# Self-attention over ragged batches on one core: V projected by key blocks, second halves that project one class lower, one class more, and a table for the SP queue

## The chip, the cores and the metric

The kernel runs on one core of a Trainium2 chip. The time is the device time of one launch in microseconds, the median of the runs shown. Before the change it is 361.95 us, the median of three runs from 361.56 to 365.25 us. Engines are called as the profile calls them: PE is TensorE's matmul, PEld its weight load, DVE VectorE, ACT ScalarE, POOL GpSimd, SP SyncE, which here only issues DMAs.

## The reference

Thirty-two batches of up to 512 rows with 512 features have a length each, drawn between 64 and 511. Rows past the length come out as zero. Eight heads of 64 features attend within a batch.

```python
for b in range(batch):                       # 32
    seq_len = lengths[b]
    x_b = x[b, :seq_len]
    q, k, v = np.split(x_b @ w_qkv, 3, axis=-1)          # w_qkv: 512 x 1536
    # heads of 64: (8, seq_len, 64) each
    scores = scale * q @ k.transpose(0, 2, 1)
    attn = exp(scores - max); attn = attn / (attn.sum(-1) + 1e-08)
    output[b, :seq_len] = (attn @ v).transpose(1, 0, 2).reshape(seq_len, 512)
```

## The kernel before, in words

The lengths are in device memory, so the program is compiled for any of them. At its start it sorts the batches by length, longest first, and takes them in sixteen pairs. Each pair gets a class, which is the smallest multiple of 32 from 64 to 512 that holds its longer batch. For every class N there is one compiled body for a whole pair (`make_body`), written out instruction by instruction for PE, ACT and DVE, and `loops` lays the bodies one behind the other: each engine compares the class of the next pair with k, and runs body k as often as the class repeats, or jumps past it. T is the number of 128-row tiles, the ceiling of N / 128.

With the lengths of this case (502, 447, 446, 436, 363, ... 75) the pairs of before have the classes 512, 448, 384, 352, 352, 352, 320, 288, 256, 224, 224, 192, 160, 160, 128 and 96. So there are four batches of four tiles, twelve of three, twelve of two and four of one.

A body has two halves, h = 0 and 1, one for each batch of the pair. In half h the kernel attends in batch h and at the same time projects the next batch, which has the buffers g = 1 - h (`half`). The order of work in a half is a string of tokens in `ORDER`, or `DENSE` for a three-tile class with 3N up to 1024. Each token issues one group of matmuls on PE and the instruction that empties their PSUM bank:

- S: scores of one head pair, `scores` (D: all three key tiles at once, `scores_dense`). Two heads of a pair have 64 rows of the array each. ACT takes the exponential into `ep`. Head pairs 1, 2 and 3 of batch h come first, and pair 0 of the next batch last, so the first scores of a half have been made in the half before.
- Q, K, B: projection of q, k or both for one head pair of the next batch (`qk`): four matmuls of N columns for each. A capital lets DVE copy the result into `qkT`, a small letter lets ACT do so.
- V: projection of v (`vproj`): for one head pair, for all T tiles, four matmuls of 128 columns per tile. DVE multiplies by the row mask into `v_aug`.
- A: attention times v, `attnv`, 128 rows of the batch at a time, 65 columns each; DVE follows with the reciprocal and the multiplications into `onat`.
- O, P: ACT stores one half of the output columns. SP stores the other where there is no P.

Projections alternate between two PSUM banks (`pa`, banks a0 and a1), scores between two others (s0 and s1). PE acquires a bank by a semaphore that the emptying instruction raises. The matmuls of a pair are 2 x 256 for four tiles, 2 x 176 for three (184 where dense), 2 x 112 for two and 2 x 52 for one; with 168 in the prologue and 8 in a bridge ahead of the one-tile classes these are all 4896 of the trace, so that every half can be found in it by counting.

The SP queue carries, for each half (`body` under `block.sync`): wait until `xT[h]` is free, T transposes of `x16[h]` into `xT[h]`, wait for the cast, the load of the batch five ranks ahead as T x 128 rows, zero fills of output rows, and for three and four tiles the second output store. The batch number comes from register loads of `idx` (`batch_of`). POOL casts `x_nat` to `x16` and writes the column of ones in `v_aug`.

`fetch_far` gives PE a hint, ahead of time, whether the next class's body will run or be jumped past.

Of the kernel before, what the change touches and what calls it, by code (L numbers as in the profile page):

```python
# [9 lines left out]
I32 = mybir.dt.int32  # L10
AF = mybir.ActivationFunctionType
ALU = mybir.AluOpType
# [7 lines left out]
CLASSES = [32 * k for k in range(16, 1, -1)]  # L20
# [34 lines left out]


class Matmuls:


    def __init__(self, mms, raises):  # L60
        self.todo = [(mm, raises.get(k, [])) for k, mm in enumerate(mms)]

    def __call__(self, e):
        for mm, sems in self.todo:
            ins = mm(e)
            for sem in sems:
                ins.then_inc(sem, 1)

# [39 lines left out]
def kernel(  # L108
# [51 lines left out]
    cls = sb("cls", [1, B // 2 + 1], I32)  # L160
    idx = sb("idx", [1, NR], I32)
    n_s = sb("n_s", [P, NR], FP32)
# [28 lines left out]
    s_cls = sem("s_cls")  # L191
    s_x0 = [sem(f"s_x0{t}") for t in range(NT)]
# [15 lines left out]
    s_xtf = [sem(f"s_xtf{h}") for h in range(2)]  # L208
    s_x16f = [sem(f"s_x16f{h}") for h in range(2)]
# [19 lines left out]
    def close(pr, b, eng, mms):  # L229
# [4 lines left out]
        pr.add("pe", Matmuls(mms, raises))  # L234
# [124 lines left out]
    def vproj(pr, bank, h, i, T):  # L359
        b = f"a{bank}"  # L360
        mms = []
        if T == 1:
# [14 lines left out]
        for t in range(T):  # L377
            for c in range(NC):
# [14 lines left out]
                in1=now[0][:, 0, 0:T].unsqueeze(2).unsqueeze(3).broadcast_to([P, T, 2, HD]),  # L393
                op=ALU.mult,
# [3 lines left out]
    def attnv(pr, h, i, T, late=False):  # L398
# [46 lines left out]
        def recip():  # L445
            pr.take("dve", full[("av", "dve")])
            pr.add("dve", lambda e: e.reciprocal(out=rv, in_=den).then_inc(s_r, 1))  # L447

        def mult():
            for j in (0, 1) if T == 1 else (i // 2,) if T != 4 or i % 2 == 0 else ():  # L450
                pr.take("dve", s_od[h][j], 16)
            pr.take("dve", s_r)

# [35 lines left out]
    def spread_last(pr):  # L489
# [14 lines left out]
    }  # L504
    DENSE = "D Q0 K0 A0 V0 D Q1 A1 k1 V1 D Q2 K2 A2 V2 D Q3 A3 k3 V3 O"

    ahead = {}

    def read_class(pr, h):
        if h == 0:  # L510
            for g in ("pe", "act", "dve"):
                pr.add(g, lambda e: next_class(e))

    def fetch_far(pr, h, N):

        k = CLASSES.index(N)
        if h == 0 and k + 2 < len(CLASSES):

            def hint(e):
                cur, far = regs[e.engine][1], regs["far"]  # L520
                e.reg_alu(far, cur, k + 2, ALU.is_lt)
                ahead[k + 1] = e.mark_branch_hint_location(far)

            pr.add("pe", hint)

    def half(pr, h, T, N, st):

        g = 1 - h
        pr.signals += [s_vf[g]] if T == 1 else [s_xtf[h], s_vf[g]]
# [7 lines left out]
        if T == 1:  # L537
            start_proj()
            qk(pr, st["bank"], g, [(i, 0) for i in range(NPAIR)], N, P)
            qk(pr, st["bank"] ^ 1, g, [(i, 1) for i in range(NPAIR)], N, P, "act")  # L540
            read_class(pr, h)
            pr.take("pe", s_on[h])
            attnv(pr, h, 0, 1)
            vproj(pr, st["bank"], g, 0, 1)
            fetch_far(pr, h, N)
            acquire(pr, f"a{st['bank'] ^ 1}")
            pr.signals.append(s_xtf[g])
            scores(pr, h, g, 0, 0, 1, N)
            act_store(pr, h, 0, T)
# [5 lines left out]
        dense = T == 3 and 3 * N <= 2 * MAXS  # L555
        toks = (DENSE if dense else ORDER[T]).split()
        for tok in toks:
# [3 lines left out]
            if k == "S":  # L561
                i, kt = units.pop(0)
                scores(pr, st["slot"], g if i == 0 else h, i, kt, T, N)
                st["slot"] ^= 1
            elif k == "D":
                i = units[0][0]
                del units[:T]
                scores_dense(pr, g if i == 0 else h, i, N)
# [9 lines left out]
            elif k in "OP":  # L578
                act_store(pr, h, "OP".index(k), T)
            else:  # L580
                start_proj()
                eng = "act" if k.islower() else "dve"
                if k == "V":
                    vproj(pr, st["bank"], g, i, T)
                elif k in "Bb":
                    qk(pr, st["bank"], g, [(i, 0), (i, 1)], N, 256, eng)
# [660 lines left out]
```

## Time and profile before

| | |
|---|---|
| median of the runs | 361.95 us |
| profiled execution, span | 359.8 us, granted clock 0.995 |
| median less span | 2.15 us |
| PE busy | 341.4 us, 4896 matmuls |
| DVE busy | 232.2 us |
| ACT busy | 228.3 us |
| POOL busy | 60.8 us |
| DMA | 76.18 MB, mean 212 GB/s |
| last matmul | starts at 352.70 us, ends at 352.90 us |
| last output store issued | 353.79 us, lands at 357.5 us |

The profiled execution is one run; its span goes from the first to the last instruction, and what is launched around it is the 2.15 us of the third row. A share of busy time is a mean over stages. A line of a group says how long its instructions ran and, behind the bar, how long the engine was idle ahead of them and who ended that. In the table by stretches each engine has its busy time in that stretch, with the count of instructions in brackets.

### The profile page before, as it was taken

The page shows a single profiled execution, that of the slowest core. Times are in us where ns is not written, and L with a number is a line of the kernel's source. Part 1 is how long each engine was busy: PE and PEld are TensorE (multiplying, and loading weights), DVE is VectorE, ACT ScalarE, POOL GpSimd, SP SyncE. Part 2 cuts the span into 40 slices and gives each one's busy share as a digit, 9 for nine tenths or more (in the row PEclk, how much of TensorE's full clock was granted, in tenths as well). Part 3 has the DMA queues.
Part 4 walks back from the last instruction along what each step waited for, and adds up shares of the span by engine and source line. Part 5 has one row for each costly group of instructions (what it writes and reads, how often), then busy time and mean ns, then how long its engine had stood idle before and what let it go on. Part 6 is the DMA issues. An engine that isn't in the chain of part 4 may idle for free. (4 is left out here: it accounts for less than half of the span.)

```text
span 359.8 us, 12852 instructions
## 1 busy us (share of the span) xinstructions
PE 341.4 (95%) x4896; PEld 246.9 (69%) x4897; DVE 232.2 (65%) x534; ACT 228.3 (63%) x299; POOL 60.8 (17%) x90
## 2 busy tenths in 40 slices
PE   6999999899989999999999999999999999999892
PEld 2566556566656667666666677788879898888761
DVE  3666666566657677676676766576756666676562
ACT  4668778677757667666676667666666565555441
POOL 2614010202010111011011011101112112212120
PEclk9999999999999999999999999999999999999997
DMA  6968998769668766989759749878896856887664
GB/s 196 379 175 272 220 298 229 195 203 171 207 166 237 192 221 202 238 254 293 215 156 318 226 120 305 263 163 192 210 237 180 162 181 161 208 164 215 169 167 111
DMA packets 85127, 76.18 MB, mean 212 GB/s; under 512 B 41552, under 2 KB 64080, under 8 KB 85072
## 3 DMA queue, kind: packets, MB, share of 16 engines
q1 hardware_dynamic: 69952, 60.78, 66.0%
q10 hardware_dynamic: 15120, 14.68, 12.6%
q8 instruction: 33, 0.54, 0.6%
q14 instruction: 22, 0.18, 0.2%
HBM read 29.37 MB, written 36.70 MB: 184 GB/s over the span
## 5 line engine op out<-in xcount | busy, mean ns | idle before, releaser
L290 ACT ACTIVATE ep<-psc 128x704 f16<-128x704 f32 (+4 forms) x217 | 173.9, 852 | 73.8 <-PE psc L248 54.7
L248 PE MATMUL pa<-xT,w_r 128*128 128x352 f16 (+11 forms) x1056 | 164.5, 284 | 1.6 <-DVE qkT L709 0.5
L357 DVE CAST qkT<-pa 128x352 f16<-128x352 f32 (+5 forms) x152 | 85.3, 562 | 58.5 <-PE pa L248 56.6
L248 PEld LDWEIGHTS pa<-xT,w_r 128*128 128x128 f16 x1056 | 82.5, 98 | 45.1 <-issue 19.3
L248 PE MATMUL pa<-w_r,xT 128*128 128x128 f16 (+1 forms) x1296 | 94.9, 221 | 2.1 <-DVE v_aug L390 1.7
L248 PEld LDWEIGHTS pa<-w_r,xT 128*128 128x128 f16 x1296 | 77.2, 98 | 18.1 <-issue 6.3
L248 PE MATMUL pav<-v_aug,ep 128*128 128x65 f16 x1792 | 79.8, 194 | 3.5 <-issue 2.9
L248 PEld LDWEIGHTS pav<-v_aug,ep 128*128 128x128 f16 x1792 | 72.1, 98 | 15.9 <-issue 4.5
L390 DVE TENSOR_TENSOR v_aug<-pa,masks 128x384 f16<-128x384 f32 (+2 forms) x116 | 60.8, 524 | 34.1 <-PE pa L248 29.8
L248 PE MATMUL psc<-qkT 64*128 64x352 f16 (+12 forms) x688 | 66.2, 292 | 1.2 <-PEq L48 1.0
L471 DVE SCALAR_TENSOR_TENSOR onat<-pav,masks,rcp 128x256 f32<-128x256 f32 (+2 forms) x128 | 51.8, 444 | 6.0 <-DVEq L48 1.9
L1119 POOL CAST v_aug<-masks 128x24 f16 (+4 forms) x33 | 9.1, 275 | 267.6 <-POOLq L900 267.6
L1114 POOL CAST x<-x_nat 128x1536 f16<-128x1536 f32 (+3 forms) x33 | 42.1, 1274 | 11.1 <-POOLq L900 10.5
L322 ACT ACTIVATE ep<-psc 128x960 f16<-128x960 f32 (+1 forms) x32 | 28.0, 928 | 16.0 <-PE psc L248 13.5
L248 PEld LDWEIGHTS psc<-qkT 64*128 64x128 f16 x688 | 23.0, 94 | 19.0 <-issue 9.4
L355 ACT CAST qkT<-pa 128x320 f16<-128x320 f32 (+4 forms) x36 | 17.4, 482 | 27.4 <-ACTq L48 17.3
L447 DVE RECIPROCAL rcp<-pav 128x8 f32<-128x8 f32 (+1 forms) x68 | 14.5, 214 | 13.5 <-PE pav L248 10.0
L469 DVE TENSOR_TENSOR onat<-pav,rcp 128x512 f32<-128x512 f32 (+2 forms) x32 | 17.8, 558 | 1.1
L658 PE MATMUL psc<-zt 128*128 128x512 f16 x22 | 6.7, 456 | 1.7 <-DVE zt L1179 1.7
L1125 POOL MEMSET ep<- 128x1024 f32 x6 | 5.4, 955 | 7.4 <-DVE x L719 7.4
L728 ACT CAST w_r<-w_f 128x512 f16<-128x512 f32 (+1 forms) x6 | 4.4, 758 | 3.3 <-DMA w_f<-in_w_qkv_dram 3.3
L658 PEld LDWEIGHTS psc<-zt 128*128 128x128 f16 x22 | 2.3, 113 | 4.3 <-issue 1.7
(58 smaller groups left out, 31.7 us busy)
## 6 DMA issues: line engine op xcount, KB each, us to landing
out_dram<-zt SPq DMA_DIRECT2D x16, 768.0 KB, 6.2
x_nat<-in_x_dram SPq DMA_DIRECT2D x12, 768.0 KB, 5.1
x_nat<-in_x_dram SPq DMA_DIRECT2D x7, 1024.0 KB, 6.7
out_dram<-onat ACTq DMA_DIRECT2D x28, 256.0 KB, 3.7
x_nat<-in_x_dram SPq DMA_DIRECT2D x12, 512.0 KB, 4.2
out_dram<-onat ACTq DMA_DIRECT2D x12, 384.0 KB, 3.3
out_dram<-onat SPq DMA_DIRECT2D x12, 384.0 KB, 3.6
x_nat<-in_x_dram SPq DMA_DIRECT2D x12, 256.0 KB, 3.7
```

The lines of the kernel that those rows point to most:

```text
L248: return lambda e: e.matmul(o, lhsT, rhs, start=start, stop=stop)
L290: lambda e: e.activation(out=dst, in_=src, func=AF.Exp, scale=scale),
L322: lambda e, par=par, b=b: e.activation(out=ep[:, i, par, 0:3, 0:N], in_=psc_f[:, par, 0 : 3 * N].rearrange("p (t n) -> p t n", n=N), func= ...
L355: group(pr, b, eng, mms, lambda e: e.copy(out=dst, in_=src))
L357: group(pr, b, eng, mms, lambda e: e.tensor_copy(out=dst, in_=src))
L390: lambda e: e.tensor_tensor(out=v_aug[h][:, 0:T, 2 * i : 2 * i + 2, 0:HD], in0=pa[:, bank, 0 : T * P].rearrange("p (t a d) -> p t a d", a= ...
L447: pr.add("dve", lambda e: e.reciprocal(out=rv, in_=den).then_inc(s_r, 1))
L469: ins = e.tensor_tensor(op=ALU.mult, **ops)
L471: ins = e.scalar_tensor_tensor(scalar=now[0][:, 1, t : t + 1], op0=ALU.mult, op1=ALU.mult, **ops)
L658: e.matmul(psc[:, 1, 0, :], zt16[:, 0:P], zt16[:, 0:MAXS], start=True, stop=True)
L1114: e.tensor_copy(out=x16[h][:, 0:T, :], in_=x_nat[h][:, 0:T, :]).then_inc(s_xc[h], 1)
L1119: e.tensor_copy(out=v_aug[h][:, 0:T, :, HD], in_=src[:, 0, 0:T].unsqueeze(2).broadcast_to([P, T, NH]),).then_inc(s_on[h], 1)
```

## The change

1. **V by key blocks.** A V token of two and more tiles calls `vtile`: one key tile, all eight heads, four matmuls of 512 columns. There are T tokens V in a half in place of four.
2. **Halves that project a class lower.** A second half exists twice: `stay` projects the next batch with N columns, and `leave` with W columns, W being the next lower entry of `CLASSES`. Where W has fewer tiles than N, the last tile's V is split among the tokens that are left. PE reads the class one pair ahead.
3. **A class of 340 rows**, for which three key tiles (1020 columns) fit the dense form. The pair of 323 and 315 rows, 352 before, is of that class. A class of 64 is there too.
4. **New orders** in `ORDER[3]`, `ORDER[2]` and `DENSE`, with more copies on ACT; in the two-tile order both A0 and A1 follow one another, and SP stores the second output half, later (`pay`).
5. **Laying of the code**: `graph` replaces `loops` for PE, ACT and DVE. A class is laid out as lead, first half, second half for staying ("again"), second half for leaving ("last"), tail. Heads are put at fixed slots of blocks of 256 instructions for PE (`addr_align`), and the three-tile first half is cut so that the branch on "stay or leave" comes inside it.
6. **SP**: a table `steps`, written by POOL at the start, has for each rank the batch ahead, the class, the own batch and a flag; one register load reads the four. There are special bodies for two tiles (`steady`) and one tile (`staged`: the transposes go to other columns of `xT` early, and POOL copies them into place).
7. **Loads of x** fetch N rows: one DMA for the full tiles and one for the remaining rows.
8. In the last half ACT issues the store ahead of its last exponentials. The reciprocal, not the multiplication behind it, waits for the earlier store.

```diff
-CLASSES = [32 * k for k in range(16, 1, -1)]
+STEP = 32
+STAGE = 256
+FIRST = {4: 20, 3: 30, 2: 20, 1: None}
+AGAIN = 60
+SECOND = {4: 20, 3: 60, 2: 0, 1: None}
+PIECE = 222
+DENSE_ROWS = 340
+CLASSES = sorted([STEP * k for k in range(2, 17)] + [DENSE_ROWS], reverse=True)
...
+    def vtile(pr, bank, h, i, T, of):
+        t = min(i, T - 1)
+        w = D // (of - T + 1) if t == T - 1 else D
+        lo = w * (i - t)
+        b = f"a{bank}"
+        mms = [
+            mm(pa[:, bank, 0:w], xT[h][:, c, t * P : (t + 1) * P],
+               w_r[:, c, 2 * D + lo : 2 * D + lo + w], c == 0, c == NC - 1)
+            for c in range(NC)
+        ]
...
     ORDER = {
...
-        3: "S S Q0 A0 K0 S S V0 Q1 A1 S S K1 V1 S S Q2 A2 K2 S S V2 Q3 A3 S S K3 V3 O",
-        2: "S S V0 B0 A0 b1 A1 V1 S S B2 V2 A2 O A3 R3 X3 V3 b3 P",
+        3: "V1 S S k0 A0 q2 S S q0 Q1 A1 S S q3 V2 S S k2 K1 S S O A2 k3 A3 S S V0",
+        2: "S S B0 b1 A0 A1 B2 S S V1 b3 A2 O A3 R3 X3 V0",
     }
-    DENSE = "D Q0 K0 A0 V0 D Q1 A1 k1 V1 D Q2 K2 A2 V2 D Q3 A3 k3 V3 O"
+    DENSE = "D V0 V2 A0 D Q0 K0 A1 k1 q1 D K2 V1 O q2 D A2 A3 k3 Q3"
...
-                scores(pr, st["slot"], g if i == 0 else h, i, kt, T, N)
+                scores(pr, st["slot"], *((g, i, kt, T, W) if i == 0 else (h, i, kt, T, N)))
...
-                    qk(pr, st["bank"], g, [(i, 0), (i, 1)], N, 256, eng)
+                    qk(pr, st["bank"], g, [(i, 0), (i, 1)], W, 256, eng)
...
-            half(pr, h, T, N, st)
+            half(pr, h, T, N, (N, W)[h], st, last and h == 1)
...
-        for b in banks:
-            acquire(pr, b)
+        acquire(pr, "a0")
+        acquire(pr, "s1")
         pr.signals.append(s_xtf[0])
         scores(pr, 1, 0, 0, 0, 1, P)
...
-    bodies = {N: make_body(N) for N in CLASSES}
+    stay = {N: make_body(N, N) for N in CLASSES}
+    lower = dict(zip(CLASSES, CLASSES[1:] + CLASSES[-1:]))
+    leave = {N: make_body(N, lower[N]) for N in CLASSES}
+    final = {N: make_body(N, lower[N], True) for N in CLASSES if N <= P}
...
+    def graph(e, name, opening=None, before=None):
...
+        for k, N in enumerate(CLASSES):
+            T = -(-N // P)
+            open_(label(k, "lead"))
+            hint_mid(k)
+            align(N, FIRST)
+            e.br(label(k, "first"))
+            open_(label(k, "first"))
...
+            if fetch:
+                stay[N].run_part(e, 0, cut(k) or stay[N].second[name], entry)
+            else:
+                stay[N].run_half(name, e, 0)
...
+                br = e.br_cmp(cur, k, label(k, "again"), out_, "IS_EQ")
+                again(k)
+            for at in mids[k]:
+                br.branch_hint(at)
...
+            open_(label(k, "last"))
+            if fetch and not rest(k, then=ahead):
+                body = leave[N]
+                body.run_part(e, body.second[name], None, ahead)
+            else:
+                leave[N].run_half(name, e, 1)
+            e.br(label(k, "tail"))
+            tail(k, hinted[0] if hinted else None)
...
+            def load(h, off, N, bi=None):
+                bi = batch_of(e, rank, tmp, off) if bi is None else bi
+                full, more = divmod(N, P)
...
+                if full:
+                    e.dma_start(
+                        out=x_nat[h][:, 0:full, :], in_=rows[:, 0:full, :]
+                    ).then_inc(s_xl[h], 16)
+                if more:
+                    e.dma_start(
+                        out=x_nat[h][0:more, full, :], in_=rows[0:more, full, :]
+                    ).then_inc(s_xl[h], 16)
...
+            def read_step(h):
+                e.reg_load(steps_r[h], steps[
+                    0:1, bass.ds(e.snap(rank, min_val=0, max_val=B - 1), 1), :])
+
+            def steady(N):
...
+                for h in range(2):
+                    if h:
+                        read_step(h)
+                    wait_dec(e, s_xtf[h])
+                    to_xT(h, N, 2)
+                    if h == 0:
+                        pay_owed(f"{N}e", False)
+                    else:
+                        pay(0)
+                    wait_dec(e, s_xc[1 - h])
+                    load(1 - h, 5, N, index(h, 0))
...
+            e.wait_ge(s_cls, 1)
+            e.tensor_copy(out=steps[:, :, 0], in_=idx[:, 5 : B + 5]).then_inc(s_steps, 1)
```

477 lines of the change are left out of this document (373 added, 104 removed), and 2 rows, old and new, of the table ORDER.

## The prediction

> **What bounds the kernel now.** First the page: busy time of each engine, then its 40 slices.
>
> ```profile
> PE 341.4 (95%) x4896; PEld 246.9 (69%) x4897; DVE 232.2 (65%) x534; ACT 228.3 (63%) x299; POOL 60.8 (17%) x90
> PE   6999999899989999999999999999999999999892
> PEclk9999999999999999999999999999999999999997
> ```
>
> PE is busy nearly everywhere, at the full clock. To see whether it streams or waits, I cut the span at the halves of the bodies (found by counting matmuls) and asked for the table by stretches. Columns: stretch, its length, busy time of PE, PEld, DVE, ACT, POOL, clock, DMA share, GB/s.
>
> ```profile
> 63.12:82.81 19.69, 18.39 (x258) 11.76 (x256) 11.72 (x25) 13.87 (x17) 2.19 (x2) 1.00 0.64 181
> 82.81:101.03 18.22, 18.22 (x258) 11.69 (x256) 12.19 (x32) 13.80 (x16) 2.20 (x2) 1.00 0.78 184
> 101.03:115.99 14.96, 13.49 (x179) 8.79 (x178) 9.35 (x19) 9.04 (x12) 1.74 (x2) 1.00 0.85 224
> 115.99:129.29 13.30, 13.30 (x178) 8.77 (x177) 8.98 (x21) 8.98 (x13) 1.74 (x2) 1.00 0.74 227
> ...
> 180.59:193.48 12.89, 12.79 (x179) 8.74 (x178) 9.12 (x20) 8.51 (x13) 1.76 (x2) 1.00 0.65 201
> 193.48:206.47 12.99, 12.84 (x179) 8.72 (x177) 8.88 (x21) 8.43 (x12) 1.73 (x2) 1.00 0.88 261
> 206.47:218.19 11.72, 11.72 (x184) 9.21 (x186) 7.69 (x17) 8.01 (x10) 1.76 (x2) 1.00 0.55 142
> ...
> 311.19:317.98 6.79, 6.36 (x113) 5.43 (x113) 4.73 (x13) 3.50 (x6) 1.30 (x2) 1.00 0.72 182
> 317.98:324.45 6.47, 6.20 (x113) 5.44 (x112) 4.31 (x13) 3.45 (x6) 1.30 (x2) 1.00 1.20 235
> 324.45:331.20 6.75, 6.36 (x114) 5.43 (x113) 4.84 (x14) 3.42 (x6) 1.30 (x2) 1.00 0.70 202
> 331.20:338.75 7.55, 6.27 (x113) 5.46 (x113) 5.10 (x14) 3.87 (x7) 1.30 (x2) 1.00 0.64 181
> ```
>
> Two things are to be seen. A half is as long as PE's stream, so fewer columns are time saved one for one. And halves with the same work differ: the first half of a class entered by a jump (448, 384) is 1.5 us longer than the second, and the halves of 160 rows (the last four) spread from 6.47 to 7.55 us. The timeline of PE shows what a jump costs.
>
> ```profile
> 65.11 0.19 PE L248 MATMUL pav<-v_aug,ep 128*128 128x65 f16 x1
> 66.59 0.39 PE L248 MATMUL pav<-v_aug,ep 128*128 128x65 f16 x7 [1.30 <-issue]
> ```
>
> The group is cut in two in its middle: no semaphore ended that wait, the instructions were not there. It is 2.2 us behind the jump over the body of 480, and 384 has 1.47 us of the same kind at 102.63.
>
> **The sum, part by part.** Everything is laid against the profiled 359.8 us. The median of the runs is 2.15 us above that, and is added at the end.
>
> 1. V by key blocks: 217 ns in place of four times 56 ns. Both pitches are on PE's timeline:
>
> ```profile
> 62.13 1.06 PE L248 MATMUL pa<-w_r,xT 128*128 128x128 f16 x16
> 344.87 1.03 PE L248 MATMUL pa<-w_r,xT 128*128 128x512 f16 x4
> ```
>
> Less the last one's own length (219 and 379 ns by the groups), (1.06 - 0.219) / 15 = 56 ns and (1.03 - 0.379) / 3 = 217 ns. That saves 7 ns for each of (1280 - 64) / 4 = 304 (the prologue keeps its 64): **2.1 us**. DVE's work hardly changes (three of 0.69 us for four of 0.56).
>
> 2. Halves that project a class lower. The slope is (217 - 56) / 384 = 0.42 ns a column. Thirteen classes are left: 512, 448, 384, 352, 340, 320, 288, 256, 224, 192, 160, 128, 96; eleven lose 32 columns, two lose 12 and 20, together 384. Q and K are 32 matmuls: 384 x 32 x 0.42 = 5.1 us. The next batch's first scores, two at a time on 64 rows each, add 0.5 us. V loses a tile of 2048 columns where the next class has a tile fewer (288 to 256, 160 to 128): 2 x 0.86 = 1.7 us. **7.3 us.** No operand is added, so nothing takes it back on PE.
>
> 3. The class of 340. One pair, at 12.89 + 12.99 us. A dense half of 320 takes 11.72 us; 20 columns more in 32 matmuls of Q and K and, at half rate, 24 of scores are 0.37 us. Two halves of 12.09: **1.7 us** less. (Term 2 has its lower second half.)
>
> 4. Body starts. The first half over the second in one class: 1.47 (448), 1.65 (384), 0.81 (288), 0.45 (second 224), 0.16 (192), 0.32 and 0.28 (160), 0.1 three times (352); and 7.55 - 6.47 = 1.08 us ahead of the bridge, which waited for all four banks and now needs two. Together 6.5 us. [...] I take **5.5 us** of it.
>
> 5. Two-tile halves. The 224 half runs 0.61 us over its bare stream (columns times 0.42, half for scores, 30 ns for a matmul of 65 columns), mostly the two turns to 64-row scores and back. The others run over that by 0.2 to 0.3 (256), 0.16 (192) and 0.5 us (160), 2.2 us together. The waits there are for `v_aug`:
>
> ```profile
> PE pa L248 <- DVE v_aug L390: 1.7, 6, 0.4
> ```
>
> The new order has two V groups for four. By the rows, at 160 columns DVE is late once more: V0's copy stands behind A3's reciprocal (0.21) and two multiplications (0.88), and ends about 1.0 us into the next half, where b1 wants its bank at 0.9. I take **1.5 us**.
>
> 6. The end: the last exponential (0.81 us) stands ahead of the store, which is issued at 353.79; the multiplication it needs ends at 353.13. **0.6 us.**
>
> Costed at nothing: the SP table, the split loads, the deferred store. SP waits long for semaphores:
>
> ```profile
> SPq L900 <- SPq L900: 91.0, 33, 8.6
> ```
>
> A second load issue is 0.4 us, a store 0.4, and the register loads get fewer. In the half of 224 at 269.02 SP's transposes run from 269.39 for 3.2 us, its load ends at 273.78, and the next half starts at 276.05: some 2 us to spare, which is the thinnest place; past that, PE pays each us. POOL's six writes of the table are like its row of 0.33 us or less and come between 18.7 us and the memset at 20.54 that waits for DVE anyway. POOL's copy into place (below the 0.61 us of its cast) has 2.3 us of idle time in each one-tile half. Six copies on ACT rather than DVE in a three-tile half: 6 x 0.45 = 2.7 us on top of 8.5, 11.2 of 12.8 us. DVE gets free, ACT gets full; laid one behind the other by the rows (exponentials 0.65 apart), each bank comes free before its next use, by 0.1 us at the tightest.
>
> What the trace doesn't show is the jump from a first half over the staying half to the leaving one: PE makes eleven of them here. From below: nothing, as the four jumps back to a loop's head (352 twice, 224, 160) cost 0.1 to 0.45. From above 1.47 each, 16 us. I take nothing, as these landings are hinted half a body ahead and fixed in their slot, and the hinted jumps of before showed no wait at the landing itself, only the later one; the nearest rows are thus those of the loops, and their tenths are in the 1.0 us kept back in term 4.
>
> Sum: 2.1 + 7.3 + 1.7 + 5.5 + 1.5 + 0.6 = 18.7. 359.8 - 18.7 + 2.15 = **343.2 us**.
>
> **Rivals.**
>
> - Code loading takes it back, and more: the slower side. PE's program gets longer (each class has two second halves) and it takes 29 branches here: 13 leads to a first half, 11 to a leaving half, 3 back, 2 over a class. At 1.39 us (the mean of the two rows) for each, 40 us are added: 383 us. It decides from fourteen stalls on, where 18.7 us are used up. For it: the two rows. Against it: the loop heads at 0.1 us. If the eleven jumps alone stall: 343.2 + 15.3 = 358.5. [...]
> - ACT is late in the six halves of 384 and 352. Each of six copies stands behind an exponential (0.65) and takes 0.45, and with 0.3 to start it is 0.2 us past the two groups (1.2 us) after which its bank is wanted: 6 x 6 x 0.2 = 7.2 us, 350.4. Against it: no such wait in dense halves, which have two copies on ACT.
> - Two-tile halves are held by SP or DVE. Term 5 is lost, and the twelve halves are each 0.3 us longer: 343.2 + 1.5 + 3.6 = 348.3.
> - It goes better: all 6.5 of term 4 and 2.2 of term 5, and 0.3 us in each of the four one-tile halves: 340.3.
>
> **Chances.** Forecast 0.62, ACT 0.12, two tiles 0.13, eleven jumps 0.06, code loading whole 0.05, better 0.02. The range reaches from 338 (better than all terms, by 2 us for the bounds of term 1 and the bridge) to 352 (past ACT and two tiles, and six of the eleven jumps): it leaves out the 0.11 of code loading and little else. A measurement of this kernel tells about 1% from no change. Faster by over 1% (below 358.3): 0.89; within: 0.06, the eleven jumps; slower: 0.05.
>
> **What would show it.** V groups of 512 columns at 217 ns, 304 of them, less the narrower ones. Second halves: 384 at 12.7, 288 at 9.9, 160 before the bridge at 5.4 us. 340's halves near 12.0 and 11.7. First halves of 448 and 384 as long as the second plus 0.5. No PE wait on "issue" over 0.5 us behind a jump. ACT about 11 us busy in a half of 352. I am wrong if PE shows gaps that end in "issue" at body changes, or waits on `qkT` from ACT, or if two-tile halves are set by the transposes.

## The result, and the profile after

The changed kernel takes 344.11 us (median of six runs, 343.62 to 345.07) against 361.56 us for the kernel before beside it (six runs, 360.79 to 365.25). The ratio is 0.9506, with a 95% interval of 0.9475 to 0.9538. Forecast were 343.2 us, from 338 to 352. The profiled execution took 344.30 us and its span is 342.5 us against 359.8, so 17.3 us are to be explained where the sum had 18.7. Medians here and below are of all runs of a kernel except one of 465.8 us at a granted clock of 0.66 (the variant without the class of 340); the ratios leave out runs well above the fastest of their kernel.

First the page of the changed kernel: busy time of each engine, PE's slices and the granted clock.

```profile
PE 330.5 (96%) x3998; PEld 203.1 (59%) x3999; DVE 200.0 (58%) x446; ACT 244.1 (71%) x343; POOL 63.7 (19%) x102
PE   7999999999999999999999999999999999999992
PEclk9999999999999999999999999999999999999997
```

There are 898 matmuls fewer, and PE is as full as before: the eights in its slices are gone. DVE gave 32 us of work away and ACT took 16 of them.

I cut this trace too at the halves of the bodies by counting matmuls. Columns of the table by stretches: stretch, its length, busy time of PE, PEld, DVE, ACT and POOL, clock, DMA share, GB/s. The rows are both halves of 448 and of 384, the second 352 half that leaves, both halves of 340, the second half of 288, and the last two halves of 160.

```profile
63.04:81.14 18.10, 18.10 (x209) 9.43 (x209) 11.59 (x25) 13.86 (x17) 2.19 (x2) 1.00 0.65 193
81.14:99.13 17.99, 17.69 (x210) 9.38 (x209) 12.28 (x34) 13.59 (x16) 2.18 (x2) 1.00 0.67 184
99.13:112.35 13.22, 13.22 (x140) 7.05 (x141) 5.41 (x11) 10.83 (x18) 1.70 (x2) 1.00 0.76 232
112.35:125.15 12.80, 12.80 (x141) 7.02 (x140) 5.70 (x13) 11.01 (x19) 1.70 (x2) 1.00 0.96 225
...
163.12:176.29 13.17, 12.64 (x142) 6.92 (x141) 6.38 (x15) 10.91 (x19) 1.70 (x2) 1.00 0.76 244
176.29:188.35 12.06, 12.06 (x149) 7.51 (x150) 6.44 (x13) 9.39 (x12) 1.76 (x2) 1.00 0.74 235
188.35:200.18 11.83, 11.78 (x149) 7.51 (x149) 6.49 (x15) 9.18 (x12) 1.76 (x2) 1.00 0.71 174
...
234.17:244.39 10.22, 9.96 (x147) 7.39 (x146) 5.56 (x15) 7.89 (x13) 1.76 (x2) 1.00 0.72 196
...
311.44:317.65 6.21, 6.11 (x89) 4.39 (x90) 4.52 (x12) 3.45 (x6) 1.30 (x2) 1.00 0.74 205
317.65:322.94 5.29, 4.88 (x89) 3.90 (x89) 3.28 (x9) 3.24 (x6) 1.30 (x2) 1.00 0.90 185
```

Against before: 448's first half 19.69 to 18.10 and 384's 14.96 to 13.22, and the first halves are now 0.11 and 0.42 us longer than the second ones, which project fewer columns, and not 1.47 and 1.65. The pair of 340 goes from 12.89 and 12.99 to 12.06 and 11.83, and the half ahead of the bridge from 7.55 to 5.29. Two rows are worse than their neighbours: the 352 half that leaves is 13.17 us long where one that stays takes 12.63, and 288's is 10.22 where 9.9 was due. Over all halves 17.2 us are saved. Around them the prologue is 0.64 longer (24.12 to 24.76 us; it varies by more than that between the profiles of one kernel's variants), and the stretch from the last matmul to the end of the span is 0.7 shorter (6.9 to 6.2).

PE waits little. These are the longest waits behind the prologue in its view of waits (what waits, on whom: us in total, times, the longest).

```profile
PE pa L292 <- PEq L57: 0.8, 2, 0.4
...
PE psc L292 <- ACT ep L334: 0.5, 1, 0.5
...
PE pa L292 <- DVE v_aug L456: 0.3, 1, 0.3
```

Before, one row alone was 1.7 us of waits for `v_aug`, and the two waits on "issue" behind the jumps (1.30 and 1.47) were 2.8 us. No wait on "issue" is left in this view. The 0.3 us on `v_aug` end the second half of 448. Of the 0.8 us in the first row, 0.41 lies behind a narrow V group in the last half of 160 and 0.37 at the head of the second half of 128 rows; both are told below. The row in the middle is the 352 half that leaves.

### The profile page after: what moved, and what is told of

Its sections match the earlier page's. It is cut to its first block, busy times and chain, and to the rows that moved or that the text cites. A ratio compares the mean times of both kernels' runs of the same rounds, so it can differ in the third digit from the quotient of the medians.

```text
span 342.5 us, 11294 instructions
## 1 busy us (share of the span) xinstructions
PE 330.5 (96%) x3998; PEld 203.1 (59%) x3999; DVE 200.0 (58%) x446; ACT 244.1 (71%) x343; POOL 63.7 (19%) x102
## 2 busy tenths in 40 slices
DMA packets 82271, 72.09 MB, mean 210 GB/s; under 512 B 40652, under 2 KB 63180, under 8 KB 82196
## 5 line engine op out<-in xcount | busy, mean ns | idle before, releaser
L334 ACT ACTIVATE ep<-psc 128x704 f16<-128x704 f32 (+7 forms) x193 | 155.6, 857 | 58.4 <-PE psc L292 43.2
L292 PE MATMUL pa<-xT,w_r 128*128 128x224 f16 (+15 forms) x1056 | 153.9, 279 | 2.2 <-PEq L57 0.8
L401 DVE CAST qkT<-pa 128x512 f16<-128x512 f32 (+9 forms) x100 | 56.2, 562 | 60.2 <-PE pa L292 59.0
L292 PE MATMUL pa<-w_r,xT 128*128 128x512 f16 (+2 forms) x384 | 83.2, 349 | 0.3 <-DVE v_aug L456 0.3
L292 PE MATMUL pav<-v_aug,ep 128*128 128x65 f16 x1792 | 76.7, 194 | 0.0
L292 PE MATMUL psc<-qkT 64*128 64x352 f16 (+17 forms) x702 | 64.9, 287 | 0.9 <-ACT ep L334 0.5
L456 DVE TENSOR_TENSOR v_aug<-pa,masks 128x512 f16<-128x512 f32 (+1 forms) x76 | 51.4, 677 | 23.5 <-PE pa L292 20.7
L366 ACT ACTIVATE ep<-psc 128x960 f16<-128x960 f32 (+3 forms) x48 | 43.1, 949 | 11.3 <-PE psc L292 9.7
L399 ACT CAST qkT<-pa 128x352 f16<-128x352 f32 (+7 forms) x88 | 39.9, 453 | 14.9 <-ACTq L57 7.4
L292 PEld LDWEIGHTS pa<-w_r,xT 128*128 128x128 f16 x384 | 31.5, 98 | 31.8 <-issue 6.0
```

Source lines behind the costliest of these rows:

```text
L292: return lambda e: e.matmul(o, lhsT, rhs, start=start, stop=stop)
L334: lambda e: e.activation(out=dst, in_=src, func=AF.Exp, scale=scale),
L366: lambda e, par=par, b=b: e.activation(out=ep[:, i, par, 0:3, 0:N], in_=psc_f[:, par, 0 : 3 * N].rearrange("p (t n) -> p t n", n=N), func= ...
L399: group(pr, b, eng, mms, lambda e: e.copy(out=dst, in_=src))
L401: group(pr, b, eng, mms, lambda e: e.tensor_copy(out=dst, in_=src))
L456: lambda e: e.tensor_tensor(out=v_aug[h][:, t, lo // HD : lo // HD + n, 0:HD], in0=pa[:, bank, 0:w].rearrange("p (a d) -> p a d", d=HD), i ...
```

## The experiments

All of these kernels compute the whole reference; none leaves work out. Each was run beside the kernel before on its chip, and the ratio is to that. Differences between a variant and the changed kernel are read from the halves of the two traces: most halves that an edit does not touch repeat within 0.1 us (single ones differ by up to 0.5, the first half of 128 by more, which is told below), while the intervals of two ratios together are some 2 us wide to either side.

### The leaving halves at full width

```diff
-    leave = {N: make_body(N, lower[N]) for N in CLASSES}
-    final = {N: make_body(N, lower[N], True) for N in CLASSES if N <= P}
+    leave = {N: make_body(N, N) for N in CLASSES}
+    final = {N: make_body(N, N, True) for N in CLASSES if N <= P}
```

> The changed kernel, but a half that leaves a class projects the next batch with the full N columns of its class (W = N) instead of the next lower entry. If columns on PE are the time, the 7.3 us of term 2 come back: 344.1 + 7.3 = 351.4 us, with the second half of 384 near 13.2, of 288 near 11.1 and of the last 160 near 6.2 us. If what a leaving half saves was lost again behind ACT, DVE or the transposes, it is under 2 us: below 346.

Measured: 348.73 us (348.48 to 350.34) beside 360.88; ratio 0.9671 (0.964 to 0.9702). That is 4.6 us above the changed kernel by the medians, 4.7 by the spans (347.2 against 342.5). Half by half the narrower projection is worth 0.48 us at 512, 0.43 at 448, 0.42 at 384, 0.19 at 352, 0.23 at 340, 0.36 at 320, 0.82 at 288, 0.35 at 256, 0.45 at 224, 0.30 at 192, 0.73 at 160, 0.45 at 128 and 0.16 at 96: 5.4 us. Then 0.6 us are given back: with narrow halves the bridge is 0.19 us longer and the first half of 128 is 0.43 us longer.

Two halves fall furthest short: 288 and 160, where a whole tile of V goes as well and 1.3 us were due. PE's timeline shows why. Here is the end of the leaving half of 288 at full width (start, us, group):

```profile
243.50 1.03 PE L292 MATMUL pa<-w_r,xT 128*128 128x512 f16 x4
244.36 0.65 PE L292 MATMUL pa<-xT,w_r 128*128 128x288 f16 x4
```

and the same place in the changed kernel:

```profile
240.41 0.60 PE L292 MATMUL pa<-w_r,xT 128*128 128x256 f16 x4
241.09 0.61 PE L292 MATMUL pa<-xT,w_r 128*128 128x256 f16 x4
241.88 0.50 PE L292 MATMUL psc<-qkT 64*128 64x256 f16 x6 [0.18 <-PEq L57]
```

The full V group of four takes 0.86 us until the next group starts. The narrow one has half the columns and takes 0.68, since the projection behind it waits for the bank that DVE copies until 241.03. That projection then takes 0.79 until the scores begin, where four matmuls of 256 columns need 0.43. The wait that ends last here is on ACT: dense scores take both score banks, and the exponentials of the scores before still hold the second one (ACT's timeline, changed kernel):

```profile
239.15 0.81 ACT L399 CAST qkT<-pa 128x256 f16<-128x256 f32 x2 [0.30 <-PE pa L292]
240.06 0.89 ACT L366 ACTIVATE ep<-psc 128x864 f16<-128x864 f32 x1
...
240.85 0.89 ACT L366 ACTIVATE ep<-psc 128x864 f16<-128x864 f32 x1
```

The last one ends at 241.74 and the scores start 0.14 us later, the same lag as at the entry to 340 (176.14 and 176.29); the profile itself names only PE's sequencer for this wait. From the scores before to these the narrow half takes 2.39 us and the full one 2.42, though the narrow one streams some 0.5 us less. In the last half of 160 the late engine is DVE. The group behind the first narrow V waits for a bank whose copy stands behind the multiplications of A1 (DVE's timeline, then PE's):

```profile
320.13 0.88 DVE L536 SCALAR_TENSOR_TENSOR onat<-pav,masks,rcp 128x256 f32<-128x256 f32 x2 [0.16 <-DVE rcp L515]
320.92 0.41 DVE L401 CAST qkT<-pa 128x256 f16<-128x256 f32 x1
```

```profile
321.48 0.61 PE L292 MATMUL pa<-xT,w_r 128*128 128x128 f16 x8 [0.41 <-PEq L57]
```

So a split V saves little: at these places PE waits for PSUM that ACT and DVE have not emptied, rather than streaming.

### Without the class of 340

```diff
-CLASSES = sorted([STEP * k for k in range(2, 17)] + [DENSE_ROWS], reverse=True)
+CLASSES = sorted([STEP * k for k in range(2, 17)], reverse=True)
...
-            for a, b in ((1, at), (at, at + 1), (at + 1, len(CLASSES))):
+            for a, b in ((1, len(CLASSES)),):
```

> The changed kernel without the class of 340: the pair of 323 and 315 rows is a third pair of 352. By term 3 of the prediction it gets 1.7 us slower: 345.8. By the halves of the changed kernel the class is worth less: with it the last half of 352 and the two of 340 take 13.17 + 12.06 + 11.83 = 37.06 us, since the dense first scores wait 0.53 us for ACT; without it they would be two staying halves of 12.63 and a leaving one of 12.63 - 0.47 = 12.16, together 37.42: 0.4 us slower, 344.5.

Measured: five runs from 344.99 to 347.51 us with a median of 346.11, beside 360.88; ratio 0.9583 (0.9553 to 0.9613). The pair's halves are 0.57 and 1.05 us longer, and the 352 half ahead of them is 0.54 shorter: in the halves the class is worth 1.1 us. (This profile's prologue is 1.36 us longer; how far the other runs share that is not known.) The 0.54 is the wait of the changed kernel's 352 half on ACT. The first scores of a dense class are three tiles at once, and they find their PSUM still held by the last exponential of the non-dense half. In this variant the same 0.5 us wait shows at the end of the second 352 half that leaves to 320; it moves with the entry to the dense classes and cannot be removed by dropping 340.

### V by key blocks with the old narrow matmuls

```diff
-            mm(pa[:, bank, 0:w], xT[h][:, c, t * P : (t + 1) * P],
-               w_r[:, c, 2 * D + lo : 2 * D + lo + w], c == 0, c == NC - 1)
+            mm(pa[:, bank, j : j + P], xT[h][:, c, t * P : (t + 1) * P],
+               w_r[:, c, 2 * D + lo + j : 2 * D + lo + j + P], c == 0, c == NC - 1)
+            for j in range(0, w, P)
             for c in range(NC)
```

> The changed kernel with the same V tokens, banks and evacuations, but each key tile's V made by sixteen matmuls of 128 columns instead of four of 512. By the two pitches (56 and 217 ns) it costs 7 ns for each of 304: 344.1 + 2.1 = 346.2 us. The rival is the code: 36 matmuls more in a three-tile half move the branches in their blocks; if that matters it is over 348. [...]

Measured: 384.78 us (382.26 to 387.54) beside 360.88; ratio 1.0668 (1.0615 to 1.0721). The matmuls themselves explain next to none of it. The 224 halves that no stall touches go from 6.96 to 7.02 us: +0.06 where eight matmuls of 512 columns became 32 of 128, which is 8 x 7 ns. Term 1's price is thus right there (the halves of 192 and 160 get 0.00 to 0.06 longer). The rest is PE waiting, 1.1 to 3.8 us at a time, nearly always for nothing that the profile shows. On its timeline, at the end of the first half of 512:

```profile
44.24 1.03 PE L292 MATMUL pa<-xT,w_r 128*128 128x512 f16 x4
49.05 1.03 PE L292 MATMUL psc<-qkT 64*128 64x512 f16 x4 [3.78 <-issue]
```

There are ten such waits, 25.5 us together, all at the end of a half: behind both halves of 512 and 448, and behind the second halves of the three-tile classes. This variant has twelve matmuls more in each full V group on PE, and the slots, the cut and the lead of the hints were left as they were. So it is these waits that cost here and not the matmuls: about 40 us, with the slower clock behind them (granted clock 0.96 in the mean, 0.994 in the changed kernel). That they come from the laying of the code is inferred; which of slots, cut and lead would be at fault is not separated.

### Without the fixed slots

```diff
-            if fetch and slot is not None:
+            if fetch and slot is not None and False:
```

> The changed kernel without the fixed slots of code heads in the blocks of 256 instructions; hints and order as they are. If the slots are what took the waits on missing instructions away, landings fall anywhere in a block, and of some sixteen far jumps a third to a half waits about 1.4 us: 350 to 355 us, with PE gaps that end in issue some microseconds behind class changes. If the hints alone do it, it is 344 to 345.

Measured: 376.69 us (372.63 to 379.4) beside 361.3; ratio 1.0423 (1.0389 to 1.0457). That is over 20 us beyond the range expected. Eight waits of 0.7 to 4.6 us, 19.5 us together, stand in the profiled execution. Five first halves carry most: 384 takes 19.40 in place of 13.22, 340 16.93 for 12.06, 320 18.36 for 11.65, 288 12.93 for 11.04, 512 21.07 for 19.38; 256's second half takes 10.92 for 7.18. Again a group is cut in its middle (the same half of 384, PE's timeline):

```profile
111.69 0.29 PE L292 MATMUL pav<-v_aug,ep 128*128 128x65 f16 x4
116.61 0.93 PE L292 MATMUL pav<-v_aug,ep 128*128 128x65 f16 x14 [4.62 <-issue]
```

The stall comes after 96 of the half's 140 matmuls, eight behind the branch on stay or leave; in 340 and 320 the first one comes at that branch itself, after 92 of 148. A second one follows later in the same half of 340 and 320. The hints are all there; without the slots they are not enough.

### Without the hints

```diff
             for at in mids[k]:
-                br.branch_hint(at)
+                pass
...
-                br.branch_hint(hinted)
+                pass
```

> The changed kernel with the slots, but no branch carries a hint (the instructions that work the hint's register out stay). If a jump over the staying half finds its target not loaded, each of eleven such jumps and the two over a class wait 1.4 us or more, less what PE has queued: 355 to 365 us, which would be the slower rival seen. If what PE has loaded ahead reaches over one half body, only the two jumps over a whole class wait: 347.

Measured: 388.11 us (384.01 to 391.61) beside 361.3; ratio 1.0634 (1.0591 to 1.0678). Ten jumps now wait, by 4.85, 1.86, 1.81, 2.41, 4.89, 4.39, 2.14, 2.26, 3.66 and 3.19 us: 31.5 us, 3.1 each. Eight of them stand where a first half jumps over its staying half to the leaving one (512, 448, 384, 340, 320, 288, 256, 192), the two of 1.86 and 2.41 behind the second halves of 512 and 448, where a class is jumped over. The profiled execution is 44.4 us longer than the changed kernel's (386.9 against 342.5), 4.4 for each wait, where 355 to 365 us had been expected in all. The difference is in the windows behind a wait. PE's timeline first, then windows of two and four us (columns as above), at that jump in the first half of 384:

```profile
119.65 1.47 PE L292 MATMUL pa<-xT,w_r 128*128 128x384 f16 x8
126.01 0.82 PE L292 MATMUL psc<-qkT 64*128 64x384 f16 x4 [4.89 <-issue]
```

```profile
120.00:122.00 2.00, 1.12 (x7) 0.47 (x5) 0.68 (x2) 1.48 (x3) 0.00 (x0) 1.00 1.03 398
122.00:126.00 4.00, 0.00 (x0) 0.00 (x0) 0.00 (x0) 0.00 (x0) 0.00 (x0) 0.82 0.48 186
126.00:128.00 2.00, 1.99 (x23) 1.25 (x24) 0.00 (x0) 1.45 (x2) 0.00 (x0) 0.50 0.03 8
128.00:130.00 2.00, 2.00 (x22) 1.45 (x20) 0.00 (x0) 0.55 (x2) 0.00 (x0) 0.50 0.56 197
130.00:132.00 2.00, 2.00 (x12) 0.65 (x10) 1.31 (x3) 1.32 (x2) 0.00 (x0) 0.64 0.00 0
```

While PE waits, every engine of the table stands still, and when PE goes on, the clock is granted at 0.50 for 4 us. So part of the wait is paid a second time, by the slower clock. That holds for seven of the ten: in the 4 us behind the waits of 1.86, 1.81 and 2.41 us the clock is 1.00, and the halves of 448, which end in the last two, get 1.88 and 2.10 us longer, the waits and no more. With the same 3998 matmuls PE is busy 343.7 us in this profile and 330.5 in the changed kernel's.

The jumps back to a loop's head and those from a lead show no wait of this kind without hints (the ten are all that the trace has), and neither does the leaving jump of 352, 224 and 160, the classes that run more than once: their halves are as long as before. It is the jump over a staying half that has not run, the step that I took at nothing, that needs its hint here, in eight of eleven.

### The kernel before, with slots and without hints

Would slots alone have helped before, and were its jumps hinted to any effect? Two runs. The first puts each comparison with k at a fixed slot of a block, on PE:

```diff
+            if name == "pe":
+                e.addr_align(256, offset=19, max_nops=0)
             br = e.br_cmp(cur, k, lab, out_, "IS_EQ")
```

> The kernel before with one edit: on PE each class's body starts at slot 20 of a block of 256 instructions. If the waits of 1.30 and 1.47 us in the first halves of 448 and 384, and 0.6 in 288, come from where the body lies in its block, they go: 361.6 - 3.3 = 358.3 us, and the first halves of 448 and 384 take 18.3 and 13.5 us. If they have another cause (the transposes, a register load), the time stays within 0.5 us of 361.6.

Measured: 385.35 us (381.68 to 385.91) beside 361.3; ratio 1.0626 (1.0572 to 1.0681). Neither time expected was met. There are two waits, 8.94 us at the entry to 448 and 9.71 at that to 384, in place of 1.30 and 1.47 (PE's timeline of the first):

```profile
64.33 1.06 PE L248 MATMUL pa<-w_r,xT 128*128 128x128 f16 x16
74.32 0.93 PE L248 MATMUL psc<-qkT 64*128 64x448 f16 x4 [8.94 <-issue]
```

The second takes the hints away:

```diff
-                br.branch_hint(ahead[k])
+                pass
```

> The kernel before with its branch hints taken off PE's class branches (the hint's register is still worked out). If the two waits of some 9 us at the jumps to 448 and 384 in the kernel before with a slot edit came from hints that no longer worked, the same two jumps now wait as long: 361.3 + 18 to 22 = 380 us. If a jump without a hint costs what it does in the changed kernel without hints (4.5 us each with the slow clock behind it), it is 370. If the hints did nothing in the kernel before, 361.

Measured: 371.74 us (370.55 to 373.36) beside 362.17; ratio 1.0283 (1.0233 to 1.0333). Waits of 2.67 and 2.52 us at the entries to 448 and 384, of 1.24 once more 2 us after the second, and the clock low behind them, here behind the first (table by stretches):

```profile
67.67:71.50 3.83, 3.83 (x42) 2.46 (x44) 0.60 (x2) 1.73 (x2) 2.20 (x2) 0.61 0.34 70
```

In the halves of 512 (second), 448 and 384 (first) that is 7.7 us for two jumps, 3.9 each, beside the 4.4 of the changed kernel without hints; the medians differ by 9.6, and this profile's prologue is 1.8 us longer too. It also shows that the slots made something worse than hints that are off: 9 us is more than three times the wait of one missed jump. Why, no run here shows. What is shown is that one half of this scheme put into the old layout costs 24 us.

### Dense order with V ahead of the scores

The 0.53 us wait on ACT at the entry to the dense classes asks for something to stand ahead of the first dense scores.

```diff
-    DENSE = "D V0 V2 A0 D Q0 K0 A1 k1 q1 D K2 V1 O q2 D A2 A3 k3 Q3"
+    DENSE = "V0 D V2 A0 D Q0 K0 A1 k1 q1 D K2 V1 O q2 D A2 A3 k3 Q3"
```

> The changed kernel with the dense order begun by V0 instead of D (V0 D V2 A0 D ...). If PE's wait of 0.53 us ahead of the first dense scores is for ACT's last two exponentials of the non-dense half, a V of 0.87 us covers it: 0.5 us faster, 343.6. If the wait only moves to the second D of each dense half, which then has 0.87 us less ahead of it, the six dense halves pay for it: no gain or up to 1 us slower.

Measured: 349.33 us (347.58 to 351.03); ratio 0.9697 (0.967 to 0.9723). The 352 half gets 0.71 us shorter, and the six dense halves 0.57 to 0.93 longer, 4.7 us together, where 1 us was the most expected. The wait has only moved to the second dense scores, six times (timeline of PE in the second half of 340, and the row of its waits):

```profile
190.51 0.72 PE L292 MATMUL pav<-v_aug,ep 128*128 128x65 f16 x18
191.82 0.61 PE L292 MATMUL psc<-qkT 64*128 64x340 f16 x8 [0.59 <-ACT ep L366]
```

```profile
PE psc L292 <- ACT ep L366: 3.2, 6, 0.7
```

Here a dense exponential needed two V groups and an attention behind its scores before the next ones: with one V group the six waits are 3.2 us. The order of the change pays 0.5 us once for that.

### Loads of whole tiles

```diff
             def load(h, off, N, bi=None):
+                N = -(-N // P) * P
```

> The changed kernel with x loaded as whole tiles of 128 rows, one DMA, instead of the rows of the class in two. I costed the loads at nothing, since they land two halves ahead: 344.1 within 0.4 us. If transfers stand in each other's way, the larger loads delay transposes and stores: 1 to 3 us slower. If the second DMA issue costs SP time that PE waits for, up to 1 us faster.

Measured: 344.48 us (344.16 to 344.57) beside 361.3; ratio 0.9527 (0.9501 to 0.9552). It moves 74.57 MB where the changed kernel moves 72.09: the loads that fetch the rows of the class alone take 2.5 MB from the queues and nothing from the time.

### All copies of the three-tile halves on DVE

```diff
-        3: "V1 S S k0 A0 q2 S S q0 Q1 A1 S S q3 V2 S S k2 K1 S S O A2 k3 A3 S S V0",
+        3: "V1 S S K0 A0 Q2 S S Q0 Q1 A1 S S Q3 V2 S S K2 K1 S S O A2 K3 A3 S S V0",
```

> The changed kernel with the copies of q and k in the non-dense three-tile halves all on DVE (capitals in that order). By the rival of the prediction, ACT with 11 of 12.7 us full would be late and this is faster by up to 7 us. By the trace no matmul waits there for ACT's copies, and DVE's queue gets six copies of 0.52 us more, with the last V's copy behind A3's multiplications: no gain, up to 2 us slower; and the first dense scores, which wait 0.53 us for ACT, wait less.

Measured: 345.76 us (344.28 to 347.57) beside 362.17; ratio 0.9543 (0.9502 to 0.9584). The halves of 384 and 352 are as long as with six copies on ACT, each within 0.1 us. ACT is not late there, and neither is DVE. The first dense scores still wait 0.53 us, so the copies are not what they wait for. The first half of 128 is 1.35 us longer, as PE waits 1.72 us there, and this edit does not touch that half. The runs fall into two groups, three from 344.3 to 344.75 and three from 346.8 to 347.6; the profile is of the slowest one, and that the first half of 128 parts the groups is not shown.

### SP a little slower

Where is SP's thin place? Four register loads in place of one add some 0.9 us to SP in each half.

```diff
-                e.reg_load(steps_r[h], steps[
-                    0:1, bass.ds(e.snap(rank, min_val=0, max_val=B - 1), 1), :])
+                for _ in range(4):
+                    e.reg_load(steps_r[h], steps[
+                        0:1, bass.ds(e.snap(rank, min_val=0, max_val=B - 1), 1), :])
```

> The changed kernel with each register load from SP's table made four times over: 0.31 us each, 0.9 us more in SP's chain of every half. In the two-tile halves SP waits 0.7 to 1.8 us for PE, and the transposes land about 1.5 us ahead of their use, so I expect 344.1 within 0.5 us. If SP is the thin place that the prediction named, the twelve two-tile halves get up to 0.9 us longer each: up to 355.

Measured: 347.59 us (346.86 to 348.05) beside 362.17; ratio 0.9594 (0.9551 to 0.9638). Eleven of the twelve two-tile halves do not move, and one of 192 is 0.28 us longer. Both halves of 128 move: 3.77 to 5.38 and 2.92 to 4.54 us, 3.2 of the 3.5 lost. In the first, PE waits for its transposed rows (timeline of PE):

```profile
329.27 2.12 PE L292 MATMUL pa<-xT,w_r 128*128 128x96 f16 x32 [1.98 <-PEq L57]
```

The second half's loss is the clock behind that wait: 0.68 in the two us from 329.27 and 0.50 in the next two. In the changed kernel the same chain is on the path already, by 0.37 us. Its links are on SP's queue, on POOL's timeline and on PE's:

```profile
320.07 0.89 SPq L1113 DMA_DIRECT2D out_dram<-onat  x1
322.52 1.19 SPq L1324 DMA_TRANSPOSE xT<-x  x1
324.24 0.40 SPq L1113 DMA_DIRECT2D out_dram<-onat  x1
```

```profile
326.47 0.61 POOL L1519 COPY xT<-xT 128x512 f16<-128x512 f16 x1 [1.69 <-POOLq L1105]
```

```profile
327.23 1.52 PE L292 MATMUL pa<-xT,w_r 128*128 128x96 f16 x32 [0.37 <-PEq L57]
```

The last two-tile half's deferred store is issued at 320.07 and its issue takes 0.89 us; the transposes are issued at 322.52 and land at 326.21, 3.7 us later; POOL copies them into place until 327.08; PE starts at 327.23. To this chain the narrower last half of 160 loses part of its gain: PE comes earlier and waits. But the chain's longest link, the landing, scatters from run to run, and the first half of 128 follows it:

| variant | transposes, issue to landing, us | first half of 128, us |
|---|---|---|
| without hints | 2.42 | 3.33 |
| leaving halves at full width | 2.63 | 3.34 |
| without slots | 3.31 | 3.34 |
| changed kernel | 3.69 | 3.77 |
| without the class of 340 | 3.95 | 4.01 |
| SP slower | 4.34 | 5.38 |
| copies on DVE | 4.51 | 5.12 |

The kernel before has 3.33 us there. So with SP slower, 0.65 of the 1.6 us that the first half loses are the landing's, and only the rest is SP's. What makes the landing scatter no run here shows.

### The deferred store behind the next transposes

If the store at 320.07 is in the way, it can stand behind the transposes.

```diff
                     elif T == 2:
-                        pay(0)
+                        e.reg_mov(kept, steps_r[0][2])
+                        e.reg_mov(owed0, 1)
...
             def pay_owed(name, clear):
+                e.br_cmp(owed0, 1, lab, out_, "IS_EQ")
+                ...
+                wait_dec(e, s_of[0][1])
+                store(e, e.snap(kept, min_val=0, max_val=B - 1), 0, 1, 2)
+                e.reg_mov(owed0, 0)
```

> The changed kernel with one SP store moved: in the last two-tile pair the second output half of the first batch is stored after the next pair's first transposes instead of ahead of them. If the first one-tile half (3.77 us, 0.44 longer than before; 5.1 to 5.4 in the two runs above) is held by the chain SP's store, table read, transposes, landing, POOL's copy, then it falls to about 3.3 us, and so does its scatter: 343.6 us, 0.5 faster than the changed kernel, or the same by the interval. If the landing itself scatters (3.7 to 4.5 us from issue), the store is not the cause, and the half stays at 3.7 us or more.

Measured: 347.81 us (346.59 to 348.38) beside 360.87; ratio 0.9631 (0.9603 to 0.9658). That is 3.7 us slower than the changed kernel, which was not expected. The first half of 128 does fall to 3.33 us; but its transposes land in 3.31 us where they took 3.69, so the store's part in it is not shown. The second half goes from 2.92 to 5.79. DVE's timeline shows who waits now:

```profile
328.38 0.21 DVE L515 RECIPROCAL rcp<-pav 128x8 f32<-128x8 f32 x1 [3.25 <-DVEq L57]
...
329.41 0.74 DVE L414 TENSOR_SCALAR v_aug<-pa,masks 128x512 f16<-128x512 f32 x1
```

The reciprocal carries the wait for the earlier store, which is now issued at 323.70 and lands at 328.24. V's copy stands behind it on DVE, its bank comes free late, and PE waits 2.69 us. The store's place and the wait's place belong together.

## Why the prediction was right

The time was forecast to within 0.9 us (the spans miss the sum by 1.4), but two terms were too large and one place was overlooked, and two terms were too small.

- **Term 1, V by key blocks, 2.1 us: held as far as it can be seen.** V's 512-column matmuls run at the pitch of the row of before, and 32 narrow matmuls in place of eight cost 0.06 us more in a 224 half. V alone in the kernel before was not tried.
- **Term 2, narrower leaving halves, 7.3 us: mis-sized, 4.6.** The sentence "nothing takes it back on PE" failed. The columns of q, k and scores are worth 0.2 to 0.5 us a half where 0.45 was due, but the tile of V that goes was to give 0.86 us twice and gave less than half of that, because behind the split V groups PE waits for PSUM: in 288 for ACT's exponentials, in 160 for a copy on DVE. And 0.6 us are lost again at the bridge and in the first half of 128, 0.4 of it in the wait for transposes.
- **Term 3, the class of 340, 1.7 us: mis-sized, 1.1 in its halves.** The halves came out as worked out, 12.06 and 11.83 for 12.09 and 11.7. Left out was what the entry to a dense class asks of ACT: 0.53 us.
- **Term 4, body starts, 5.5 us: held, and a little more.** The first halves of 448, 384, 288 and the second 224 are 1.59, 1.73, 1.05 and 0.55 us shorter, 4.9 together, of which 0.3 is V's gain of term 1. The last half of 160, at full width, takes 6.03 us like the other one, so its 1.08 ahead of the bridge are gone, and so are the 0.3 of 352. That is 5.9. The three starts of 192 and 160 can't be told from term 5; at full width these first halves are still 0.15 to 0.20 us longer than the second ones. No wait on "issue" is left behind a jump. That 5.5 of the 6.5 us would go was my estimate, and no run shows that share; the traces show the 5.9.
- **Term 5, two-tile halves, 1.5 us: small.** At full width the ten halves of 256, 224 (first pair), 192 and 160 are 4.4 us shorter than before. Less the 1.08 at the bridge and 0.56 of V's own gain, 2.8 are left for this term and the three starts, which had 0.76 of what was seen. Both changes are in the same halves, and the new order alone in the kernel before was not tried; so their parting is argued, not shown.
- **Term 6, the end, 0.6 us: held,** 0.7.
- **Costed at nothing.** The loads are worth nothing, as measured. The six copies on ACT cost nothing: ACT is 10.5 to 11 us busy in a half of 384 or 352, as forecast, and no bank is late there. "Some 2 us to spare" on SP was right for the two-tile halves, but they were not "the thinnest place". That is the entry to the one-tile classes, where store issue, transposes, and POOL's copy follow one another. I compared POOL's copy with POOL's idle time and not with the chain that it lengthens. It cost 0.4 us at the first half of 128, and 3.2 more with 0.9 us more on SP and a landing that was 0.65 slower.
- **The jumps at nothing: right, but on thinner ice than the text had it.** The price of a missed jump was given as 1.39 us, from two rows that were waits some way behind a hinted landing. A jump that stalls without its hint costs 4.4 us in the mean, 3.1 of wait and the rest of slow clock (granted clock 0.952 in the mean, 0.994 in the changed kernel). So the rival of code loading decides at 18.7 / 4.4, about four misses and not fourteen, and its whole price is 44 us without the hints and 33 without the slots, either of which makes the kernel slower than before. The rival lost because hints and slots together leave no wait at any jump, which the trace of before could not show. Without hints eight of the eleven jumps stalled and two others. That PE waits there for its instructions is inferred: the waits end in "issue" and appear when hints or slots alone are taken away, and no view shows the loading itself.

With the terms as measured (2.1 + 5.4 + 1.1 + 5.9 + 2.8, less 0.6 at the bridge and the entry to 128) the halves would save 16.7 us; they save 17.2, and 0.5 us I can't assign. The rival in which ACT is late in 384 and 352 falls with the copies moved to DVE (ACT is late once in the leaving half of 288), and the one in which two-tile halves are held by SP falls with the slower SP. The misses of terms 2 and 3 and the gains of 4 and 5 nearly cancel: the total is better than the steps, and that is luck.

## What to carry to other kernels

Where PE streamed without gaps here, fewer columns were time one for one only as long as the engines that empty PSUM kept up (0.82 us of the 1.3 due came at 288, 0.73 at 160); where a group is cut short, follow the copies and exponentials that its next bank waits for, not the stream. Specialised code for every case paid here with every jump ahead both hinted early and landed at a fixed slot (344.11 us, against 388.11 without the hints and 376.69 without the slots); the price of one miss (4.4 us here) should be measured before the plan rests on none. Helper copies and stores on idle engines are to be checked against the chain that they lengthen at the change from one kind of body to the next, not against the engine's idle time.

## What the runs showed of the hardware

- A wait of PE behind a jump cost more than itself in seven of the ten cases without hints: behind waits of 2.14 and 4.89 us the granted clock was 0.57 and 0.50 for some 4 us, and behind waits of 1.81, 1.86 and 2.41 us it was 1.00. In the kernel before without hints it was 0.61 for 3.8 us behind a wait of 2.67 us. Over the ten waits, 31.5 us, the span grew by 44.4 us, about 40% more.
- A jump back over a pair's body, some 280 matmuls in a pair of 352, cost PE 0.1 us or less without any hint, and a jump ahead over half a body 1.8 to 4.9 us in the eight of eleven that stalled.
- Twelve matmuls more in each full V group, with the slots, the cut and the lead of the hints left as they were, came with ten waits of 1.1 to 3.8 us, 25.5 together, at the ends of three- and four-tile halves.
- The transposes of one batch of 128 rows landed 3.7 us after their issue at the entry to the one-tile classes, and between 2.4 and 4.5 us in the variants; at 3.31 us and less PE did not wait for them there, at 3.69 it did, by 0.37.
